# Score products over 128 rows, and a later place for one group of splits in the passage to the feed-forward

## The chip, the cores and the metric

The kernel runs on one core of a Trainium2 chip. The core has five engines with an instruction stream each: TensorE (PE in the profile; its weight loads are listed as PEld), VectorE (DVE), ScalarE (ACT), GpSimd (POOL) and SyncE (SP, which here only issues DMAs). They wait for each other by semaphores. The metric is the device time of one execution in microseconds (us), lower is better; the time of a kernel is the median over its runs.

## The reference, cut to what matters

One layer of a hybrid encoder, for 1024 new tokens behind 16 learned meta tokens (one sequence) and 32 further tokens with a cache of 256. A token mixer has three parts (forgetting attention with 6 heads of 64, pooling, a state-space scan), whose outputs go through one output projection; then comes a gated feed-forward. The change touches the scores of the attention and the start of the feed-forward:

```
def fox_block(q, k, v, c_q, c_k, q_pos, k_pos):
    s = jnp.einsum('bqhd,bkhd->bhqk', q, k).astype(jnp.float32) * (HD_FOX ** -0.5)
    s = s + jnp.transpose(c_q, (0, 2, 1))[:, :, :, None] - jnp.transpose(c_k, (0, 2, 1))[:, :, None, :]
    p = jax.nn.softmax(jnp.where(mask, s, -jnp.inf), axis=-1)
    return jnp.einsum('bhqk,bkhd->bqhd', p.astype(v.dtype), v)
...
    h = rmsnorm(x, ln_pre_ffn)
    ff = (jax.nn.silu(h @ w_gate) * (h @ w_up)) @ w_down
```

All is float32.

## The kernel before

**Split numbers.** TensorE multiplies in a format (fp32r) that keeps fewer bits than float32. So every operand is split into a high part (ScalarE copies it with rounding) and a low part (VectorE or GpSimd subtracts the high part from the original), and a product of two matrices is three products: high by high, high by low, low by high (`PASSES`).

**Scores.** A head has 64 channels, so the scores of a head contract over 64 rows only. The kernel stacks the parts: `K` holds the keys' high part in rows 0 to 63 and their low part in rows 64 to 127; `Q` holds the queries' high part in both halves. One product `Q` by `K` over 128 rows thus gives high by high and high by low together. The third term, queries' low part `QL` by the keys' high part, is a second product over 64 rows. `prep(h)` loads a head's operands into one tile `H` by ten DMAs of SyncE (keys, queries, `QL`, the bias `bc`, the values V) and counts up the planner's guess of when they have landed.

**One head** has 9 tiles of queries (48 rows, then eight of 128 rows), whose keys are cut into chunks of at most 512 columns: 15 chunks a head, 90 in all. For a chunk `s_products` issues the first product (`s`, 128 rows), then for a chunk that touches the diagonal a product that adds the mask (`am`, 128 columns or what of them lies in the chunk), and last the second product. VectorE adds the bias and takes the minimum (`s_min`, line 1029), ScalarE takes the exponential (`s_exp`, line 1040), TensorE transposes the result (`t`, line 1075), ScalarE and VectorE split it (`PT`, lines 58 and 63), TensorE multiplies by V (`o`), ScalarE evicts (`ot`).

**Order.** The loop over the chunks records, in each of its turns, one chunk's products, one group of transposes, the products of an earlier group, and then as many products of other work as a planner's clock allows: first the projections of the following heads (`wk`), later partial sums of the output projection (`wp`). The planner's clock, the guessed arrivals of DMAs and the `yield`s of `prep` fix the order of all five engines when the kernel is built; at run time each engine only works off its stream, in that order.

**The passage.** After the output projection the first two units of the feed-forward are computed with products that need no sums of weights (`first_units`, tiles `gc` and `gd`), while the last tokens are still normalised, transposed (`c_turns`) and split into the slots of `T`. `prep()` splits the next weight: ScalarE the high part, VectorE the low part. `c_parts(off, n)` splits `n` columns of the second half of the tokens (two splits) and forms two differences of the blocks (`c_diffs`, lines 1350 and 1351). The last weight of unit 1 is split into a place in `H2`, a tile of a pool that is opened there; its reader is the second half of `rows(1, 1, 0)` (`gc<-T,H`). `wx` is the weight before it, and `gd` are the products of the same units with the second half of the tokens.

Of the kernel before, what the change touches and what calls it, by code (L numbers as in the profile page):

```python
# [15 lines left out]
P = 128  # L16
D = 1024
NK = 8
NT = 1072
# [3 lines left out]
KEYS = PAST + NT  # L23
# [27 lines left out]
def tile_hybrid_trunk(ctx: ExitStack, tc: tile.TileContext, a: dict):  # L51
# [16 lines left out]
    def mm(out, lhsT, rhs, start, stop):  # L68
        return nc.tensor.matmul(out, lhsT, rhs, start=start, stop=stop, skip_group_check=True)  # L69
# [28 lines left out]
    def psum(tag, name):  # L98
        return where.get(tag, psp[0]).tile([P, 512], F32, tag=tag, bufs=PSB[tag], name=name)
# [14 lines left out]
    qd = [dr.tile([2, P, NT], F32, name=f"qd{p}") for p in range(3)]  # L114
# [7 lines left out]
    cd = dr.tile([6, KEYS], F32, name="cd")  # L122
# [110 lines left out]
    for t in range(9):  # L233
        R, o = TROW[t], TOFF[t]
# [4 lines left out]
        ps = zps[t]  # L239
# [98 lines left out]
    def cv_tile(tag, name):  # L338
        return CV.tile([P, EW], F32, tag=tag, bufs={"ext": 2, "cv": 4}[tag], name=name)
# [53 lines left out]
    for b in range(3):  # L393
        c0, n = CH[b]
        ps = psum("sm", f"ft{b}")
        for t in CTILES[b]:
            R, c = TROW[t], TOFF[t] - c0
# [47 lines left out]
    for i in range(5):  # L445
# [9 lines left out]
        h = cv_tile("cv", f"ch{i}")[:, :W]  # L455
# [19 lines left out]
    def arrival(nbytes):  # L475
        queue[0] = max(queue[0], clock[0]) + nbytes / 330.0
        return queue[0] + LATE[0]
# [333 lines left out]
    live, n = [], 0  # L811
# [27 lines left out]
    def prep(h):  # L839
        pr, hb = h // 2, 64 * (h % 2)  # L840
        H = (HB if h % 2 else HA).tile([P, HW], F32R, tag="H", name=f"H{h}")

        K, Q, QL = H[:, :KEYS], H[:, KEYS:KEYS + NT], H[:64, KEYS + NT:KEYS + 2 * NT]
        bc = H[:, KEYS + 2 * NT:2 * KEYS + 2 * NT]
        V = H[:, 2 * KEYS + 2 * NT:HW - P].rearrange("p (t c) -> p t c", c=P)
        Vm = H[:, HW - P:]
        heads[h] = (Q, QL, K, V, Vm, bc)
        v = vd[pr][:, h % 2].rearrange("r d j -> r (d j)")
        hs = slice(hb, hb + 64)
        loads = [(K[:64], kd[pr][0, hs]), (Q[:64], qd[pr][0, hs]), (K[64:], kd[pr][1, hs]), (Q[64:], qd[pr][0, hs]),  # L850
                 (QL, qd[pr][1, hs]), (bc, cd[h].partition_broadcast(P)),
                 (V[:, 0:2], v[0:PAST].rearrange("(t p) c -> p t c", p=P)), (V[:48, 2], v[PAST:PAST + 48]),
                 (Vm, v[PAST + 48 - P:PAST + 48]),
                 (V[:, 3:], v[PAST + 48:].rearrange("(t p) c -> p t c", p=P))]
        for i, (dst, src) in enumerate(loads):
            sync.dma_start(dst.bitcast(F32), src)
            at = arrival(4 * P * (KEYS if i == 5 else NT if i == 9 else KEYS // 2))
            if i % 2:
                yield
        ready[h] = at  # L860
# [113 lines left out]
    def geom(t):  # L974

        return TROW[t], TOFF[t], (0 if t == 0 else PAST + NS), (304 if t == 0 else NM + P * t)
# [13 lines left out]
    def place(t):  # L990

        free = [i for i in ring if SW[i] >= PAD + geom(t)[3]]
        return free[-1] if free else None

    def s_products(h, u, t, j, nch):
        Q, QL, K, V, Vm, bc = heads[h]
        R, o, k0, Lk = geom(t)
        if j == 0:
            st = AT.tile([P, 4], F32, tag="st", bufs=6, name=f"st{h}_{t}")
            i = place(t)  # L1000
            ring.remove(i)
            tiles[h, t] = (Sring[i], st)
            slot[h, t] = i
            if t in (0, 1, 3, 5, 7):
                i = 2 * ((5 * h + u) % 4)
                rows[h, u] = rsum[:, i:i + 2]
        j0 = 512 * j
        n = min(512, Lk - j0)
        ps = psum("s", f"s{h}_{t}_{j}")
        ks = slice(k0 + j0, k0 + j0 + n)  # L1010
        mm(ps[:R, :n], Q[:, o:o + R], K[:, ks], True, False)
        if t == 0:
            mm(ps[:R, :n], identr[:R, :R], am0, False, False)
        else:
            d0 = max(Lk - P, j0)
            d1 = j0 + n
            if d1 > d0:
                mm(ps[:R, d0 - j0:d1 - j0], identr, am[:, d0 - (Lk - P):d1 - (Lk - P)], False, False)
        mm(ps[:R, :n], QL[:, o:o + R], K[:64, ks], False, True)
        return ps  # L1020

    def s_min(h, u, t, j, nch, ps):
# [101 lines left out]
    while ti < len(Tgroups) or tolo or toprod or toout or later:  # L1124
# [31 lines left out]
        if tv:  # L1156
            for hi, lo, v in tv[1]:
                hi_of(hi, v)
            h, u, g, ng = tv[0]
# [8 lines left out]
        if s:  # L1168
            s_min(*s[0], s[1])
            h, u, t, j, nch = s[0]  # L1170
# [148 lines left out]
    def h_block(q):  # L1319
        return HT[:, q].rearrange("p (k n) -> p k n", k=4)  # L1320
# [19 lines left out]
    def c_parts(off, n):  # L1340

        for b in range(2):
            x = h_block(2 * b + 1)[:, :, off:off + n]
            split(*[t_slot(4 + 2 * b + j)[:, :, off:off + n] for j in range(2)], x)
        c_diffs(off, n)

    def c_diffs(off, n):

        b11, b12, b22 = [h_block(q)[:, :, off:off + n] for q in (0, 1, 3)]
        dv.tensor_tensor(out=b11, in0=b12, in1=b11, op=SUB)  # L1350
        dv.tensor_tensor(out=b12, in0=b22, in1=b12, op=SUB)
# [13 lines left out]
    def split(hi, lo, raw, eng=None):  # L1365
        hi_of(hi, raw)
        (eng or dv).tensor_tensor(out=lo, in0=raw, in1=hi.bitcast(F32), op=SUB)  # L1367
# [4 lines left out]
    def t_slot(m):  # L1372

        return T[:, m % 2, 4 * (m // 2 % 2):4 * (m // 2 % 2) + 4, CHN * (m // 4):CHN * (m // 4) + CHN]
# [67 lines left out]
    at = {"prep": 0, "raw": 0, "load": 0}  # L1442
# [121 lines left out]
    for t in range(9):  # L1564
        ks = (3, 4) if t < 2 else (0, 1, 2, 3, 4)
# [39 lines left out]
    def part_psums(nm):  # L1605

        turns[0] += 1
        return [psum(("mm", "sm")[turns[0] % 2], f"{nm}_{h}") for h in range(2)]
# [10 lines left out]
    def classic(f, q, ps, c, last):  # L1619

        w = W["gu", f, -(2 * q[0] + q[1] + 1)]
        for h in range(2):
            s = PART[h]
            n = s.stop - s.start
            for k in range(4):
                for j, (i0, i1) in enumerate(PASSES):
                    o = t_slot(4 * c + 2 * q[1] + i1)
                    mm(ps[h][:, :n], w[:, i0, k * P:(k + 1) * P], o[:, k, s],
                       q[1] == 0 and k == 0 and j == 0, last and k == 3 and j == 2)
        if c:  # L1630
            used(W.pop(("gu", f, -(2 * q[0] + q[1] + 1))))
# [219 lines left out]
    def first_units():  # L1851

        def rows(f, r, c, between=None):
            ps = part_psums(f"gc{f}_{r}_{c}")
            for m in range(2):
                classic(f, (r, m), ps, c, m == 1)
                if between and not m:
                    between()
            return ps

        for _ in range(3):
            prep()
        c_norms(9)
        prep()
        gate = rows(0, 0, 0)
        c_parts(0, 144)
        c_turns(7)
        prep()
        prep()
        up = rows(0, 1, 0)  # L1870
        c_norms(10)
        c_parts(144, 128)
        prep()
        classic_out(m1, gate, up)
        nc.gpsimd.dma_start(actd[0, :, 0], m1)
        gate = rows(1, 0, 0, lambda: c_turns(8))
        c_parts(272, 128)
        C.release()
        FX = tc.alloc_tile_pool(name="FX", bufs=1, side="right")
        H2pool[0] = FX  # L1880
        H2[0] = FX.tile([P, 6, SLOT], F32R, name="H2")

        w8 = H2[0][:, 5, :1024].rearrange("p (j c) -> p j c", j=2)
        places.append(w8)
        once.append(w8)
        prep()
        up = rows(1, 1, 0)
        classic_out(u2, gate, up)
        nc.gpsimd.dma_start(actd[1, :, 0], u2)
        ps = {(f, r): part_psums(f"gd{f}_{r}") for f in range(2) for r in range(2)}  # L1890
        b12, t1, t2, t3, t4, b22 = [act_out(0, i) for i in (0, 5, 6, 7, 4, 3)]
        for m in range(2):
            for f in range(2):
                for r in range(2):
                    classic(f, (r, m), ps[f, r], 1, m == 1)
                    if m and r:
                        classic_out((b12, b22)[f], ps[f, 0], ps[f, 1])
                        if f == 0:
                            dv.tensor_tensor(out=t1, in0=b12, in1=m1, op=SUB)
                    next(hgen)  # L1900
                    prep_more()
        dv.tensor_tensor(out=t2, in0=b22, in1=t1, op=SUB)
        dv.tensor_tensor(out=t3, in0=b22, in1=b12, op=SUB)
        dv.tensor_tensor(out=t4, in0=u2, in1=t2, op=SUB)
        nc.gpsimd.dma_start(actd[2, :, 0], t1)
        nc.gpsimd.dma_start(actd[3:7, :, 0].rearrange("s p n -> p s n"),
                            HT[:, 3].rearrange("p (s n) -> p s n", n=CHN))
# [205 lines left out]
```

## Time and profile before

| what | value |
|---|---|
| median of 3 runs | 1263.66 us (1263.57 to 1264.64) |
| the profiled execution, its own time | 1267.12 us |
| its span in the profile | 1265.3 us |
| granted TensorE clock, mean | 0.988 |
| TensorE busy with products | 1224.8 us (97% of the span) |
| VectorE busy | 843.5 us (67%) |
| ScalarE busy | 501.0 us (40%) |
| DMA queue of SyncE | 191.57 MB, 47.0% of 16 engines' span |

"Busy" is the time in which an engine has at least one instruction under way. A product's duration in the profile overlaps with the next one's, since products are pipelined, so what one costs is read from the start of one to the start of the next. In a timeline row the first number is the start, the second the time that the merged instructions span; `128*128 128x512` is a weight of 128 rows by 128 columns, moved over by 512 columns. What stands in brackets is the engine's idle time before, if it is over 0.15 us, and what ended it ("issue": nothing that the profile shows). The attention lies between 240 and 472 us of the span, the passage between 547 and 622 us.

### The profile page before, as it was taken

The numbers are of one execution on the slowest core, as the hardware profiler recorded it, in microseconds if no ns is written. First come the engines' busy times: TensorE is split into PE (matmuls) and PEld (weight loads), VectorE is DVE, ScalarE is ACT, GpSimd is POOL, SyncE is SP. The second block draws the span as 40 slices with busy tenths as digits, with TensorE's granted clock in tenths as the row PEclk, the third lists the DMA queues.
The fourth block names the chain that finished last, engine by engine and source line by source line (L and its number), as shares of the span: only waits on it lengthen the run. The fifth ranks groups of instructions, "written<-read, shape, count | busy, mean of one in ns | idle before, by whom it ended". The sixth has DMA issues, their size and how long they took to land.

```text
span 1265.3 us, 22956 instructions
## 1 busy us (share of the span) xinstructions
PE 1224.8 (97%) x8780; PEld 1146.1 (91%) x8780; DVE 843.5 (67%) x1620; ACT 501.0 (40%) x1104; POOL 193.2 (15%) x303
## 2 busy tenths in 40 slices
PE   7999899999999999889899999999999999999997
PEld 6999888888877776679899999999999999999996
DVE  4488687267676455675877777777777767555576
ACT  7422254245466562552432323223232335444432
POOL 0100386200122342440000000000000000000022
PEclk9999999999989999998999999999999999999998
DMA  9421264766665836551243444344433578655544
GB/s 299 148 82 55 63 175 151 243 199 182 200 193 174 262 109 229 201 168 67 77 137 138 171 145 162 133 151 154 167 128 137 196 273 302 243 187 181 186 145 148
DMA packets 128478, 213.85 MB, mean 169 GB/s; under 512 B 16227, under 2 KB 82857, under 8 KB 128369
## 3 DMA queue, kind: packets, MB, share of 16 engines
q1 hardware_dynamic: 123056, 191.57, 47.0%
q0 software_dynamic: 5312, 20.82, 4.3%
q8 instruction: 69, 1.13, 0.4%
q14 instruction: 41, 0.33, 0.1%
HBM read 144.66 MB, written 67.69 MB: 168 GB/s over the span
## 4 chain that ended last, share of the span: by engine, by line
PE 49%; DVE 1%; DMA 0%; issue 0%; ACT 0%; DVEq 0%; ACTq 0%
PE dn L69 14%; PE gy L69 14%; PE gz L69 9%; PE gx L69 9%; PE dl L69 3%; PE eT L1801 0%; DMA wsd<-ws 0%; DVE H L1367 0%; DVE ey L1831 0%; DVE HD L1367 0%; PE eT L1814 0%; DVE ey L1816 0%; DVE m L1663 0%; DVE T L1367 0%; DVE HT L1693 0%
## 5 line engine op out<-in xcount | busy, mean ns | idle before, releaser
L69 PE MATMUL wk<-T,wkh 128*128 128x384 f32 (+1 forms) x1152 | 205.2, 330 | 1.5 <-POOL wkh L66 0.8
L69 PEld LDWEIGHTS wk<-T,wkh 128*128 128x128 f32 x1152 | 186.8, 189 | 4.8 <-POOL wkh L66 1.1
L69 PE MATMUL gx<-T,HD 128*128 128x272 f32 (+1 forms) x960 | 120.5, 285 | 2.3 <-ACT m L1642 2.3
L69 PEld LDWEIGHTS gx<-T,HD 128*128 128x128 f32 x960 | 118.4, 188 | 2.5 <-ACT m L1642 2.5
L69 PE MATMUL gy<-H,HD 128*128 128x272 f32 (+1 forms) x960 | 119.3, 283 | 1.4 <-DVE m L1663 1.4
L69 PEld LDWEIGHTS gy<-H,HD 128*128 128x128 f32 x960 | 117.4, 188 | 1.6 <-DVE m L1663 1.6
L1367 DVE TENSOR_TENSOR HD<-rg,HD 128x512 fp32r<-128x512 f32 x126 | 86.1, 685 | 39.3 <-ACT HD L58 39.3
L69 PE MATMUL dn<-T,HD 128*128 128x272 f32 (+1 forms) x816 | 101.0, 285 | 0.4 <-DVE m L1663 0.4
L69 PEld LDWEIGHTS dn<-T,HD 128*128 128x128 f32 x816 | 100.1, 188 | 0.7 <-DVE m L1663 0.6
L69 PE MATMUL dn<-T,W 128*128 128x272 f32 (+1 forms) x768 | 94.7, 284 | 0.2 <-DVE W L1367 0.2
L69 PEld LDWEIGHTS dn<-T,W 128*128 128x128 f32 x768 | 93.9, 188 | 0.4 <-DVE W L1367 0.4
L1663 DVE TENSOR_TENSOR m<-gy,m 128x272 f32<-128x272 f32 x120 | 51.8, 432 | 48.8 <-PE gy L69 47.5
L58 ACT ACTIVATE HD<-rg 128x512 fp32r<-128x512 f32 x126 | 74.5, 624 | 18.5 <-PE gy L69 17.8
L58 ACT ACTIVATE PT<-t 128x512 fp32r<-128x512 f32 (+2 forms) x96 | 44.7, 472 | 90.1 <-PE t L1075 35.4
L1699 POOL DMA_DIRECT2D actd<-HT x20 | 15.3, 766 | 391.7 <-DVE HT L1675 273.8
L58 ACT ACTIVATE HD<-scr 128x512 fp32r<-128x512 f32 x20 | 12.7, 636 | 154.3 <-DVE scr L1498 154.3
L63 DVE TENSOR_TENSOR PT<-t,PT 128x512 fp32r<-128x512 f32 (+2 forms) x96 | 50.1, 527 | 31.9 <-ACT PT L58 31.0
L69 PE MATMUL s<-H 64*128 64x512 f32 (+5 forms) x180 | 65.0, 373 | 0.0
L69 PE MATMUL gy<-T,HD 128*128 128x272 f32 (+1 forms) x480 | 61.8, 285 | 0.0
L69 PE MATMUL gz<-T,HD 128*128 128x272 f32 (+1 forms) x480 | 61.6, 284 | 0.0
L69 PE MATMUL gz<-H,HD 128*128 128x272 f32 (+1 forms) x480 | 61.2, 283 | 0.0
L1367 DVE TENSOR_TENSOR T<-HT,T 128x528 fp32r<-128x528 f32 (+2 forms) x83 | 57.9, 704 | 4.9 <-ACT T L58 4.9
(309 smaller groups left out, 2276.3 us busy)
## 6 DMA issues: line engine op xcount, KB each, us to landing
rg<-in_wgu_dram SPq DMA_DIRECT2D x44, 512.0 KB
HT<-actd SPq DMA_DIRECT2D x77, 264.0 KB
actd<-HT POOLq DMA_DIRECT2D x11, 1056.0 KB, 5.7
ws<-in_wd_dram SPq DMA_DIRECT2D x44, 256.0 KB
wsd<-ws SPq DMA_DIRECT2D x44, 256.0 KB
rd<-wsd SPq DMA_DIRECT2D x20, 512.0 KB
wkr<-in_wx_dram SPq DMA_DIRECT2D x16, 512.0 KB
actd<-HT POOLq DMA_DIRECT2D x10, 792.0 KB, 4.0
```

Source lines behind the costliest of these rows:

```text
L58: nc.scalar.activation(out, in_, AF.Copy)
L63: nc.vector.tensor_tensor(out=out, in0=in_, in1=hi.bitcast(F32), op=ALU.subtract)
L69: return nc.tensor.matmul(out, lhsT, rhs, start=start, stop=stop, skip_group_check=True)
L1367: (eng or dv).tensor_tensor(out=lo, in0=raw, in1=hi.bitcast(F32), op=SUB)
L1663: return lambda h, ps: dv.tensor_tensor(out=out[:, PART[h]], in0=ps, in1=other[:, PART[h]], op=ADD)
L1699: nc.gpsimd.dma_start(actd[r0:r0 + n, :, p].rearrange("s p n -> p s n"), HT[:, 2 * (p % 2) + 1 - q, CHN * s0:CHN * (s0 + n)].rearrange("p ...
```

## The change

The second product of the scores is taken over 128 rows: `QL`, the queries' low part, is loaded twice, into rows 0 to 63 and 64 to 127, and is multiplied by the whole `K` (high and low part). The result so gets the term low by low as well. That is one DMA more for each of the six heads (64 by 1072 float32), so `prep` has eleven loads, and the planner counts the time of one more. In the passage `c_parts(272, 128)` stands behind the last `prep()` of unit 1, where it stood ahead of it.

```
-        K, Q, QL = H[:, :KEYS], H[:, KEYS:KEYS + NT], H[:64, KEYS + NT:KEYS + 2 * NT]
+        K, Q, QL = H[:, :KEYS], H[:, KEYS:KEYS + NT], H[:, KEYS + NT:KEYS + 2 * NT]
...
-                 (QL, qd[pr][1, hs]), (bc, cd[h].partition_broadcast(P)),
+                 (QL[:64], qd[pr][1, hs]), (QL[64:], qd[pr][1, hs]), (bc, cd[h].partition_broadcast(P)),
...
-            at = arrival(4 * P * (KEYS if i == 5 else NT if i == 9 else KEYS // 2))
+            at = arrival(4 * P * (KEYS if i == 6 else NT if i == 10 else KEYS // 2))
...
-        mm(ps[:R, :n], QL[:, o:o + R], K[:64, ks], False, True)
+        mm(ps[:R, :n], QL[:, o:o + R], K[:, ks], False, True)
...
         gate = rows(1, 0, 0, lambda: c_turns(8))
-        c_parts(272, 128)
         C.release()
...
         prep()
+        c_parts(272, 128)
         up = rows(1, 1, 0)
```

The planner's count of arrivals moves the order of the whole attention a little. At its end, on TensorE, this is the run from the last head's last scores to the output projection; in the kernel before (`t_4_0` to `t_4_4` are the groups of transposes of the last two query tiles, `o_4` their products, `wp` the partial sums):

```order
L69 MATMUL o_3_5072<-PT_3_3_5088,H_4460 128x128 x2
L69 MATMUL wp_1_5131<-wo_3421,T 128x512 x3
L1075 MATMUL t_4_1_5135<-ident,S_2392 128x128
L1075 MATMUL t_4_1_5135<-ident,S_2390 128x128
L1075 MATMUL t_4_1_5135<-ident,S_2392 128x128
L1075 MATMUL t_4_1_5135<-ident,S_2390 128x128
L69 MATMUL wp_1_5131<-wo_3730,T 128x512 x3
L69 MATMUL wp_1_5131<-wo_3861,T 128x512 x3
L1075 MATMUL t_4_2_5154<-ident,S_2392 128x128
```

In the changed kernel the same run on TensorE reads:

```order
L69 MATMUL o_3_5095<-PT_3_3_5112,H_4468 128x128 x2
L1075 MATMUL t_4_1_5150<-ident,S_2392 128x128
L1075 MATMUL t_4_1_5150<-ident,S_2390 128x128
L1075 MATMUL t_4_1_5150<-ident,S_2392 128x128
L1075 MATMUL t_4_1_5150<-ident,S_2390 128x128
L1075 MATMUL t_4_2_5164<-ident,S_2392 128x128
```

The nine `wp` products that stood between these transposes have gone to earlier places. In the passage, on ScalarE, the kernel before has this order (`yT` are the transposed last tokens, `T<-HT` the high parts of `c_parts(272, 128)`, `H<-rg` the high part of the last weight of unit 1):

```order
L1338 ACTIVATE HT<-yT_1_6084 128x4x128
L58 ACTIVATE T<-HT 128x4x128 x2
L58 ACTIVATE H_6129<-rg_1_5742 128x512
L1637 ACTIVATE m_5891<-gc_0_0_0_6053 128x272
L1637 ACTIVATE m_5891<-gc_0_0_1_6054 128x256
```

and the changed one:

```order
L1338 ACTIVATE HT<-yT_1_6090 128x4x128
L58 ACTIVATE H_6129<-rg_1_5748 128x512
L58 ACTIVATE T<-HT 128x4x128 x2
L1637 ACTIVATE m_5897<-gc_0_0_0_6059 128x272
L1637 ACTIVATE m_5897<-gc_0_0_1_6060 128x256
```

The weight's high part is now ahead of the tokens'. On VectorE the same place reads, before (`T<-HT` the low parts, `HT<-HT` the two differences, `H<-rg` the low part of the weight):

```order
L63 TENSOR_TENSOR T<-yT_1_6084,T 128x4x128
L1367 TENSOR_TENSOR T<-HT,T 128x4x128 x2
L1350 TENSOR_TENSOR HT<-HT 128x4x128
L1351 TENSOR_TENSOR HT<-HT 128x4x128
L1367 TENSOR_TENSOR H_6129<-rg_1_5742,H_6129 128x512
```

and in the changed kernel:

```order
L63 TENSOR_TENSOR T<-yT_1_6090,T 128x4x128
L1367 TENSOR_TENSOR H_6129<-rg_1_5748,H_6129 128x512
L1367 TENSOR_TENSOR T<-HT,T 128x4x128 x2
L1350 TENSOR_TENSOR HT<-HT 128x4x128
L1351 TENSOR_TENSOR HT<-HT 128x4x128
```

The weight's low part has moved ahead of four instructions of `c_parts`.

## Rows read from the trace of the kernel before

**Rows 1.** The page's first part: busy time of each engine in us, its share of the span, and the number of its instructions.

```profile
PE 1224.8 (97%) x8780; PEld 1146.1 (91%) x8780; DVE 843.5 (67%) x1620; ACT 501.0 (40%) x1104; POOL 193.2 (15%) x303
```

**Rows 2.** Busy time by stretch, for three stretches of the attention (with `wk` products between, with none, with `wp` products between). Columns: stretch, its length, busy us and number of instructions of PE, PEld, DVE, ACT and POOL, the granted share of TensorE's clock, the mean busy share of the DMA engines, GB/s.

```profile
240.00:343.00 103.00, 103.00 (x649) 89.49 (x647) 64.92 (x166) 48.09 (x130) 12.37 (x10) 1.00 0.63 186
343.00:372.00 29.00, 27.24 (x159) 21.08 (x157) 24.14 (x61) 18.79 (x48) 7.41 (x6) 0.88 0.65 198
372.00:464.00 92.00, 92.00 (x522) 71.38 (x521) 53.48 (x130) 53.70 (x129) 28.49 (x34) 1.00 0.64 191
```

**Rows 3.** The list of waits between 235 and 465 us: who waited for whom, us in total, how often, the longest one.

```profile
DVE S L1029 <- PE s L69: 42.6, 45, 5.2
...
PEld s L69 <- issue: 11.5, 42, 0.4
...
PEld t L1075 <- issue: 7.5, 32, 0.4
...
PEld o L69 <- issue: 2.4, 10, 0.2
...
PE t L1063 <- DVE T L63: 1.0, 1, 1.0
...
PE wk L69 <- POOL wkh L66: 0.8, 1, 0.8
...
PE wk L69 <- ACT wkh L58: 0.7, 1, 0.7
PE t L1075 <- ACT S L1040: 0.7, 1, 0.7
```

**Rows 4.** The timeline of TensorE's products at the start of the fifth head: a masked chunk of 272 columns, the first chunk of 512 columns (masked over 112), and the one of 16.

```profile
394.12 0.85 PE L69 MATMUL wp<-wo,T 128*128 128x512 f32 x3
394.82 0.29 PE L69 MATMUL s<-H 128*128 128x272 f32 x1
394.94 0.22 PE L69 MATMUL s<-am,identr 128*128 128x128 f32 x1
395.09 0.39 PE L69 MATMUL s<-H 64*128 64x272 f32 x1
395.41 0.33 PE L1075 MATMUL t<-ident,S 128*128 128x128 f32 x1
...
398.36 0.39 PE L69 MATMUL s<-H 128*128 128x512 f32 x1
398.58 0.21 PE L69 MATMUL s<-am,identr 128*128 128x112 f32 x1
398.73 0.50 PE L69 MATMUL s<-H 64*128 64x512 f32 x1
399.15 0.66 PE L1075 MATMUL t<-ident,S 128*128 128x128 f32 x4
399.57 0.42 PE L69 MATMUL o<-PT,H 128*128 128x128 f32 x2
...
400.57 0.17 PE L69 MATMUL s<-H 128*128 128x16 f32 x1
400.60 0.26 PE L69 MATMUL s<-am,identr 128*128 128x16 f32 x1
400.78 0.27 PE L69 MATMUL s<-H 64*128 64x16 f32 x1
400.99 0.33 PE L1075 MATMUL t<-ident,S 128*128 128x128 f32 x1
```

**Rows 5.** The timeline at a chunk of 512 columns without a mask, weight loads included (the two products of the chunk are one row, the second starts with its weight load at 457.64).

```profile
457.09 0.19 PEld L69 LDWEIGHTS s<-H 128*128 128x128 f32 x1
...
457.32 0.82 PE L69 MATMUL s<-H 128*128 128x512 f32 x2
...
457.64 0.18 PEld L69 LDWEIGHTS s<-H 64*128 64x128 f32 x1 [0.36 <-issue]
...
458.07 0.66 PE L1075 MATMUL t<-ident,S 128*128 128x128 f32 x4
```

**Rows 6.** The weight loads of the tile of scores `s` in the view of one tile: count, shortest, median and longest duration in ns, first and last start, and their forms with counts.

```profile
L69 PEld LDWEIGHTS s<-H x180: 119/183/338, 240.2 to 460.5; 128*128 128x128 f32 x84, 64*128 64x128 f32 x84, 128*48 128x48 f32 x6, 64*48 64x48 f32 x6
```

**Rows 7.** The timeline of the passage around the last weight of unit 1 (`H<-rg`) and its reader (`gc<-T,H`).

```profile
576.28 1.14 ACT L58 ACTIVATE T<-HT 128x512 fp32r<-128x512 f32 x2
576.93 1.29 DVE L1367 TENSOR_TENSOR T<-HT,T 128x512 fp32r<-128x512 f32 x2 [1.19 <-ACT T L58]
577.32 0.61 ACT L58 ACTIVATE H<-rg 128x512 fp32r<-128x512 f32 x1
...
577.99 0.52 PE L69 MATMUL gc<-T,H 128*128 128x272 f32 x2 [0.73 <-ACT H L58]
...
578.86 0.69 DVE L1351 TENSOR_TENSOR HT<-HT 128x512 f32<-128x512 f32 x1
579.47 0.69 DVE L1367 TENSOR_TENSOR H<-rg,H 128x512 fp32r<-128x512 f32 x1
580.21 5.19 PE L69 MATMUL gc<-T,H 128*128 128x272 f32 x22 [1.70 <-DVE H L1367]
...
585.20 9.47 PE L69 MATMUL gd<-T,HD 128*128 128x272 f32 x72
```

**Rows 8.** Busy time by stretch, columns as in Rows 2, just behind that.

```profile
580.00:585.00 5.00, 4.79 (x22) 4.79 (x23) 0.60 (x2) 0.00 (x0) 0.00 (x0) 0.50 0.31 105
```

## Prediction

> **What bounds the kernel now.** I read the page's busy times first [rows 1]: TensorE has a product under way for 97% of the span, VectorE works 67% of it, ScalarE 40%. That makes TensorE the first suspect everywhere, but says nothing yet on whether its products are as dense as they could be. So I went to the attention, where the first edit lies, by stretch [rows 2]: TensorE is busy 103.00 of 103 us and 92.00 of 92 us, and VectorE there only 64.92 and 53.48. The list of waits says the same from the other side [rows 3]: between 235 and 465 us TensorE's products waited for another engine four times, 3.2 us in all, while VectorE alone waited 42.6 us for the scores. Only the stretch from 343 to 372 us, in which no foreign products fill the gaps, is different: VectorE is busy 24.14 of 29 us, and TensorE no longer all the time [rows 2]. The reader is to see that in 203 of 232 us an instruction that TensorE saves shortens the span, and in 29 us hardly.
>
> The same list shows something odd [rows 3]: the unit that loads weights stood idle ahead of loads for scores 42 times, 11.5 us, behind nothing that the profile knows ("issue"), and as oddly ahead of transposes (7.5 us) and of products by V (2.4 us). Elsewhere it loads the next weight under the running product. The timeline shows where [rows 4, 5]: each idle piece stands at the change from a product over 128 rows to the one over 64, or back.
>
> **The first edit: what a second product costs.** I take starts, not durations, and compare each step with what it takes between products of 128 rows. The references: three `wp` products of 512 columns take 0.70 us, 0.23 each; 272 columns take 0.12; and two products with a weight each are never less than about 0.11 apart, which the four transposes show (0.42 for four) [rows 4].
> - 512 columns without a mask: from the first product to the second 0.32 us, from the second to the transposes 0.43 [rows 5]. Over 128 rows I expect 0.23 each, so 0.29 less.
> - 512 columns with a mask: 0.15 from the mask to the second product, 0.42 from there on [rows 4]. Expected 0.11 and 0.23: 0.23 less.
> - 272 columns: 0.15 and 0.32 [rows 4]. Expected 0.11 and 0.12: 0.24 less. Chunks of 144 and 400 columns have the same two changes, and I price them alike.
> - 16 columns: 0.18 and 0.21 [rows 4]. Expected 0.11 twice: 0.17 less.
> - The first query tile of a head: its mask product has 48 rows and stays so, so the change of rows only moves from behind the second product to ahead of it: nothing.
>
> There are 84 second products with 64 rows by 128 columns, and 6 of the last kind [rows 6]. By the widths of the keys a head has six chunks of 512 columns, two of them masked, and two each of 16, 144, 272 and 400. So: 24 x 0.29 = 7.0; 12 x 0.23 = 2.8; 36 x 0.24 = 8.6; 12 x 0.17 = 2.0; together **20.4 us**. The idle time of the weight loads at "issue" is the same thing counted from the other side, 11.5 + 7.5 + 2.4 = 21.4 us [rows 3], and serves as the upper bound.
>
> What takes from it. (a) In the stretch from 343 to 372 us VectorE has 24.14 us of work [rows 2]. That stretch's share of the 20.4 by length is 2.6 us, which would leave 26.4 us, with VectorE busy 91% of it and itself behind ScalarE's splits. I take 2.0 of the 2.6 as lost. (b) At the end of the attention the order has taken nine `wp` products out from between the last transposes. They cost 9 x 0.23 = 2.1 us wherever they stand, but they covered the time in which the splits are made. The price lies between nothing and 2.1; I take 1.0, since ScalarE and VectorE go on splitting meanwhile. (c) The six added DMAs carry 0.27 MB each; at 186 GB/s [rows 2] that is 1.5 us of transfer a head, next to DMA engines that are 63 to 65% busy. They lie a head ahead of their use and cost the path nothing. Queued behind each on SyncE are the bias and the values of the same head and the writes of earlier results; nobody waits for a DMA in the list [rows 3]. If that cover went, it would be 1.5 us a head, 9 us in all. (d) The planner's shift moves when other products fill the gaps, not how many there are. I price it at nothing, between the 2.1 us of (b) lost once more and as much gained. So the first edit brings **17.4 us**, between 12 (20.4 less 2.6, 2.1, 1.5 for one head at (c), and 2.1) and 21.4.
>
> **The second edit.** In the passage TensorE reaches `gc<-T,H` at about 577.1 us and waits 0.73 us for the weight's high part, does two products, and waits 1.70 us for its low part [rows 7]. ScalarE makes the high part at 577.32 behind the two token splits of `c_parts`; VectorE makes the low part at 579.47 behind two token splits and two differences [rows 7]. In the new order the high part takes the tokens' place at 576.28 and ends at 576.9; VectorE follows at about 576.95 and ends at 577.64. TensorE gets to the third product at 577.3 or so and can go on at 577.7 instead of 580.21: **2.5 us**. What is late next is `c_parts` itself: 0.6 us later on ScalarE, its low parts end near 578.9 and its differences at 580.3. Their first reader is the second half of `gd`, not before TensorE has done 22 more products, 2.7 us; it is covered, and if it were not, it would cost what is missing of that, under 1 us.
>
> Then the clock. From 580 to 585 us the granted clock is 0.50, the lower of the two levels (1.2 GHz instead of 2.4) [rows 8]: 22 products take 4.99 us [rows 7], where 24 of the `gc` kind at full clock take about 0.12 each, 2.7 in all. Before it fell TensorE had stood idle for 2.4 of 3.2 us. Without these waits I expect no fall there, which gives back 2.3 us up to 585.2 and some 0.7 in `gd`, **3.1 us**. The price lies between 0 (it falls all the same) and 3.1; I take 3.1, since the idle time ahead of it is nearly gone. The second edit thus brings 5.6 us, between 2.5 and 5.6.
>
> **Sum.** The profiled execution took 1267.12 us; 17.4 + 5.6 = 23.0 less is 1244.1. It lies 3.46 us above the median of the runs, 1263.66, so against these the forecast is 1240.7, rounded **1241 us**.
>
> **Rivals.**
> 1. Row count is not what costs. The second product is also the last of its group, and the time could lie in that place, or in the reading of `H`. Against it: `wp` and `o` products that end a group show no such step [rows 4], and both the step in and the step out are there at chunks with and without a mask. For it: the weight loads of both kinds take the same time, 0.19 and 0.18 us [rows 5]. Then only the second edit is left: 1263.66 - 2.5 to 5.6, about 1259 us. Chance 0.06. The Trainium skill speaks for this rival: "TensorE: Matmul & The Clock Gate", section "LDWEIGHTS (loading the stationary operand)", says that a load's time goes by its columns and that 32 rows load as slowly as 128. By that rule alone the sum would be without its 20.4 us. The trace agrees on the loads, but not on the steps between products, and these I trust.
> 2. VectorE and ScalarE take TensorE's place. Half of the 20.4 us turns into waits of TensorE for exponentials and splits. For it: the stretch of (a). Against it: 142.5 us of VectorE work in 224 us of these three stretches [rows 2]. Gain 10.2 + 2.5: 1251 us. Chance 0.17.
> 3. Slower than before: a head's scores wait for its loads. Heads follow each other sooner while each has more to load through the in-order queue of SyncE. To eat the whole 23 us, the five heads behind the first must each wait over 4.6 us. A head's loads are 3.2 MB, 17 us at 186 GB/s [rows 2]; if 5 us of that showed at each of the five, the time would be 1241 + 25 = 1266 us. Nothing in the list waits for a load of `H` [rows 3]. Chance 0.03.
> 4. More than forecast: the low clock in the stretch from 343 to 372 us (0.88 granted of 29 us is 3.5 us lost [rows 2]) goes too, and nothing is lost at (a) and (b): 21.4 + 5.6 + 3.5 = 30.5 less, 1233 us. Chance 0.08.
>
> **How the numbers follow.** My forecast has the remaining 0.66, with a range of its own from 1236 to 1247. The range for 8 in 10 reaches from rival 4's 1233 to the bounds on the other side: 12 + 2.5 us gained and one more fall of the clock, 3.5 us, is 11 us less, 1253. That includes rival 2 and leaves out rivals 1 and 3 and what lies beyond. A measurement of this kernel can tell about 0.2%, 2.5 us, from no change. Faster by more than that are the forecast, rivals 2 and 4, and most of rival 1 (0.04): 0.95. Rival 1's rest and a little of what stands between is no change, 0.03; slower is 0.02.
>
> **What would show it.** Right: in the profile of the changed kernel the step from a second product of 512 columns to the next one is 0.23 us, not 0.42; the idle weight loads at "issue" are gone from the list; the attention ends some 17 us sooner; `gc<-T,H` runs on with under 0.5 us of waits and at full clock. Wrong: TensorE waits over 5 us in all for VectorE or ScalarE in the attention (rival 2), or for DMAs to `H` (rival 3); the steps stay over 0.4 us (rival 1); or the clock falls at other places than now, 3.5 us each.

## The result, and the profile after

| kernel | median | runs | ratio to before, 95% interval |
|---|---|---|---|
| before | 1263.84 us | 1263.57 to 1264.64 | |
| changed | 1250.08 us | 1246.46 to 1253.17 | 0.9891, 0.9869 to 0.9912 |

The change saves 13.8 us, where 22.7 were forecast: the direction is right and the time lies inside the range, but two fifths of the gain are missing, and the narrower range of the forecast itself, 1236 to 1247 us, was missed. The profiled execution (1246.46 us, span 1244.7 us, mean granted clock 0.992) is the shortest of the changed kernel's four; that of before (1267.12 us) lay above its median. Between these two the difference is 20.7 us, so what the profiles show has to be held against the medians.

First the page's busy times, as [rows 1]: TensorE has 24.5 us less of work with the same number of products.

```profile
PE 1200.3 (96%) x8780; PEld 1141.0 (92%) x8780; DVE 841.6 (68%) x1620; ACT 500.2 (40%) x1104; POOL 194.9 (16%) x303
```

The steps are gone, as forecast. In the timeline of TensorE's products in the changed kernel stand a masked chunk of 272 columns, four transposes behind a chunk of 512, a masked chunk of 512, one of 16, and (last) one of 512 without a mask, as [rows 4, 5]:

```profile
383.23 0.29 PE L69 MATMUL s<-H 128*128 128x272 f32 x1
383.35 0.22 PE L69 MATMUL s<-am,identr 128*128 128x128 f32 x1
383.41 0.34 PE L69 MATMUL s<-H 128*128 128x272 f32 x1
383.59 0.27 PE L1075 MATMUL t<-ident,S 128*128 128x128 f32 x1
...
387.74 0.60 PE L1075 MATMUL t<-ident,S 128*128 128x128 f32 x4
388.10 0.42 PE L69 MATMUL o<-PT,H 128*128 128x128 f32 x2
...
402.37 0.40 PE L69 MATMUL s<-H 128*128 128x512 f32 x1
402.61 0.21 PE L69 MATMUL s<-am,identr 128*128 128x112 f32 x1
402.65 0.45 PE L69 MATMUL s<-H 128*128 128x512 f32 x1
402.95 0.27 PE L1075 MATMUL t<-ident,S 128*128 128x128 f32 x1
...
449.06 0.17 PE L69 MATMUL s<-H 128*128 128x16 f32 x1
449.09 0.26 PE L69 MATMUL s<-am,identr 128*128 128x16 f32 x1
449.20 0.26 PE L69 MATMUL s<-H 128*128 128x16 f32 x1
449.31 0.33 PE L1075 MATMUL t<-ident,S 128*128 128x128 f32 x1
```

```profile
439.62 0.42 PEld L69 LDWEIGHTS s<-H 128*128 128x128 f32 x2
439.85 0.62 PE L69 MATMUL s<-H 128*128 128x512 f32 x2
440.09 0.58 PEld L1075 LDWEIGHTS t<-ident,S 128*128 128x128 f32 x4
440.32 0.49 PE L1075 MATMUL t<-ident,S 128*128 128x128 f32 x3
```

Read by starts: from the mask product to the transposes 0.24 us (272 columns; before 0.15 + 0.32), 0.34 (512; before 0.15 + 0.42) and 0.22 (16; before 0.18 + 0.21); from the first product of an unmasked chunk to the transposes 0.47 (before 0.32 + 0.43). In the last fence the weight loads lie under the running products again, where [rows 5] has the one for 64 rows begin only at 457.64, after 0.36 us of idle time. The idle time of the weight loads at "issue" between 235 and 465 us, 21.4 us in [rows 3], is 2.7 us here. With the counts of the prediction the starts give 24 x 0.28 + 12 x 0.23 + 36 x 0.23 + 12 x 0.17 = 19.8 us.

These starts end at the first transpose, and a part of the step lies behind it. Four transposes behind a chunk of 512 columns take 0.42 us in [rows 4] (399.15 to 399.57) and 0.36 here (387.74 to 388.10). By the medians over all chunks it is 0.04 to 0.06 us at each width but 16 columns, some 4 us more, so that the steps are worth about 24 us in all.

The waits, though, have grown. These are TensorE's own in the list of waits of the changed kernel between 235 and 465 us (who waited for whom, us in total, how often, the longest):

```profile
PE wp L69 <- ACT pp L938: 2.6, 1, 2.6
PE o L69 <- ACT ot L1113: 2.0, 4, 0.8
PE o L69 <- DVE PT L63: 1.9, 3, 0.8
PE wk L69 <- DVE k L572: 1.2, 1, 1.2
PE sT L888 <- issue: 0.9, 1, 0.9
PE wk L69 <- POOL wkh L66: 0.8, 1, 0.8
PE wk L69 <- ACT wkh L58: 0.5, 1, 0.5
PE t L1075 <- ACT S L1040: 0.5, 2, 0.2
PE t L1075 <- DVE T L63: 0.4, 1, 0.4
```

That is 10.8 us against 3.2 in [rows 3] (3.8 if the attention of before is followed to its end at 472 us). The longest is new and of a kind that the prediction did not have: TensorE waits until ScalarE has emptied a bank of partial sums into the buffer `pp`. The timeline there, DMA issues included:

```profile
398.52 0.58 ACT L938 ACTIVATE pp<-wp 128x512 f32<-128x512 f32 x1
...
412.69 0.32 SPq L940 DMA_DIRECT2D ppd<-pp  x1
...
417.79 0.60 ACT L938 ACTIVATE pp<-wp 128x512 f32<-128x512 f32 x1 [4.33 <-DMA ppd<-pp]
...
418.44 1.43 PE L69 MATMUL wp<-wo,T 128*128 128x512 f32 x3 [2.60 <-ACT pp L938]
```

ScalarE stood idle for 4.33 us, and what released it was a store of an earlier content of `pp`. There are two such buffers, so it is by their order the store issued at 412.69. What it stores was complete when the eviction of 398.52 ended: it was issued 13.6 us later, behind loads of the next head and other transfers in SyncE's stream, and freed its buffer only by 417.79, another 5.1 us later. Behind that wait the clock falls. By stretch (length, then busy us and instructions of PE, PEld, DVE, ACT and POOL, granted clock, DMA share, GB/s), first there and then in the passage:

```profile
416.00:424.00 8.00, 5.50 (x17) 4.19 (x18) 1.09 (x2) 3.15 (x8) 3.00 (x5) 0.79 0.73 254
```

```profile
560.00:568.00 8.00, 7.83 (x65) 7.61 (x64) 5.95 (x10) 3.23 (x8) 0.56 (x1) 1.00 0.29 107
```

The passage itself went as forecast. Its timeline, as [rows 7]:

```profile
561.22 0.62 ACT L58 ACTIVATE H<-rg 128x512 fp32r<-128x512 f32 x1
561.75 1.14 ACT L58 ACTIVATE T<-HT 128x512 fp32r<-128x512 f32 x2
561.88 0.69 DVE L1367 TENSOR_TENSOR H<-rg,H 128x512 fp32r<-128x512 f32 x1 [1.18 <-ACT H L58]
...
562.05 0.41 PE L69 MATMUL gc<-T,H 128*128 128x272 f32 x2
...
562.63 2.94 PE L69 MATMUL gc<-T,H 128*128 128x272 f32 x22 [0.16 <-DVE H L1367]
```

Waits of 0.73 and 1.70 us have become 0.16, and the 22 products take 2.8 us at a clock of 1.00 (562.63 to 565.41, where `gd` starts), where [rows 7, 8] had 4.99 us at 0.50.

### The profile page after: what moved, and what is told of

The parts are those of the page before. It is cut to its first block, busy times and chain, and to the rows that moved or that the text cites. A ratio compares the mean times of both kernels' runs of the same rounds, so it can differ in the third digit from the quotient of the medians.

```text
span 1244.7 us, 22979 instructions
## 1 busy us (share of the span) xinstructions
PE 1200.3 (96%) x8780; PEld 1141.0 (92%) x8780; DVE 841.6 (68%) x1620; ACT 500.2 (40%) x1104; POOL 194.9 (16%) x303
## 4 chain that ended last, share of the span: by engine, by line
PE 49%; DVE 1%; DMA 1%; issue 0%; ACT 0%; DVEq 0%; SPq 0%; ACTq 0%
PE dn L69 15%; PE gy L69 13%; PE gx L69 9%; PE gz L69 9%; PE dl L69 3%; DMA HT<-actd 1%; PE eT L1801 0%; DMA wsd<-ws 0%; DVE HD L1367 0%; DVE H L1367 0%; DVE ey L1831 0%; PE eT L1814 0%; DVE m L1663 0%; DVE T L1367 0%; DVE ey L1816 0%
## 5 line engine op out<-in xcount | busy, mean ns | idle before, releaser
L69 PE MATMUL o<-PT,H 128*128 128x256 f32 (+1 forms) x324 | 59.2, 297 | 4.1 <-ACT ot L1113 2.0
L69 PEld LDWEIGHTS gy<-T,HD 128*128 128x128 f32 x480 | 60.0, 189 | 0.0
```

## The experiments

Each time stands beside runs of the kernel before on the same chip, and the ratio is to these; one hundredth in the ratio is 12.6 us. With single ratios known to 0.1 to 0.3 hundredths, a difference of two is uncertain by some 2 to 5 us. The kernel before itself scattered more there than in the runs above, from 1259.33 to 1273.31 us, with granted clocks from 0.993 to 0.984.

| run | order | added transfer | rows | passage | median, us | ratio (95%) |
|---|---|---|---|---|---|---|
| e1 | old | yes | 128 | old | 1250.06 | 0.9875 (0.9848 to 0.9902) |
| e2 | old | no | 64 | new | 1261.72 | 0.9971 (0.9950 to 0.9992) |
| e3 | new | yes, not read | 64 | new | 1263.90 | 0.9991 (0.9973 to 1.0009) |
| e4 | old | yes | 128 | new | 1246.79 | 0.9848 (0.9820 to 0.9876) |
| e5 = changed | new | yes | 128 | new | 1249.18 | 0.9883 (0.9864 to 0.9901) |
| e6 | old | no, zeros | 128 | new | 1240.47 | 0.9821 (0.9802 to 0.9840) |
| e7 | old | yes; sums by GpSimd | 128 | new | 1243.02 | 0.9838 (0.9818 to 0.9858) |
| e8 | old | yes | 96 | new | 1247.46 | one run |
| e9 | old | no, zeros; sums by GpSimd | 128 | new | 1242.05 | 0.9828 (0.9815 to 0.9842) |
| e10 | old | yes, not read | 64 | new | 1261.79 | 0.9982 (0.9971 to 0.9992) |
| e11 | old | no, zeros | 128 | old | 1245.42 | 0.9846 (0.9832 to 0.9860) |
| e12 | old | no | 64, swapped | old | 1271.86 | one run |

The theory at the start: the steps belong to the row count and are worth what was forecast; the missing 9 us are waits that the new order brought. The rivals: the gain is the order's (rival 1), or the shorter products meet waits whatever the order (rival 2).

**e1, the 128 rows in the old order.** The second transfer is issued with the first and the planner doesn't count it, so that TensorE, VectorE and ScalarE run the order of before.

```
-            sync.dma_start(dst.bitcast(F32), src)
+            for d in ((dst, QL[64:]) if i == 4 else (dst,)): sync.dma_start(d.bitcast(F32), src)
...
-        mm(ps[:R, :n], QL[:, o:o + R], K[:64, ks], False, True)
+        mm(ps[:R, :n], QL[:, o:o + R], K[:, ks], False, True)
```

> The kernel before with the second product over 128 rows alone: queries' low part is loaded twice, but the planner doesn't count the added transfer, so that the order of TensorE, VectorE and ScalarE is that of before; the passage is as before. Theory (a change of the row count between products is what costs): the 84 steps get shorter by 20.8 us in the sum of the start-to-start times, and some 3 us come back as waits, so 1246 us against 1263.8. Rival 1 (the row count costs nothing, the new order of the changed kernel brought the gain): 1262 to 1264. Rival 2 (waits for exponentials and splits eat half of it whatever the order): 1253.

1250.06 us. The gain is not the order's: rival 1 falls. It is smaller than expected: the time lies half way between the theory (1246) and rival 2 (1253). TensorE's wait for `pp` is here too, 3.2 us.

**e2, the passage alone.**

```
-        c_parts(272, 128)
         C.release()
...
         prep()
+        c_parts(272, 128)
```

> The kernel before with the passage's edit alone. Theory: 2.5 us of waits and one fall of TensorE's clock (3 us) go, 1258 us. Rival (the fall comes all the same, a little later, or is not there in most runs of the kernel before): 1261 us.

1261.72 us, 3.2 less than the 1264.88 of before. That is nearer to the rival (2.8 less than 1263.8) than to the theory (5.8 less), but the interval, 1 to 6 us, holds both. In the profile the clock is 1.00 at the place of the edit (572 to 580 us). It falls at an earlier one instead, where that of before is at 1.00:

```profile
558.00:566.00 8.00, 6.37 (x38) 5.94 (x37) 6.23 (x10) 6.94 (x14) 3.64 (x5) 0.79 0.59 197
```

**e3, the changed kernel with 64 rows.**

```
-        mm(ps[:R, :n], QL[:, o:o + R], K[:, ks], False, True)
+        mm(ps[:R, :n], QL[:64, o:o + R], K[:64, ks], False, True)
```

> The changed kernel with its order and its eleven loads, but the second product of the scores over 64 rows again (the doubled load of the queries' low part is made and not read). Theory: the steps at the changes of the row count come back (0.42 us from a second product of 512 columns to the transposes), 20.8 us in all, of which the waits that the changed kernel shows in the attention (10 us against 3.8 before) hide some; the new order by itself costs between 0 and 3 us. So 1258 to 1262 us. Rival 1 (the gain is from the order): 1250 us as the changed kernel. Rival 3 (the new order by itself costs 6 us, the longer waits being all its own): 1264 us.

1263.90 us. The new order and the transfer eat what the passage's edit gave (0.9991 against 0.9971), 2.5 us. Row count alone separates this kernel from the changed one: 0.9991 against 0.9891, 12.6 us.

**e4, both edits in the old order** (the edits of e1 and e2 together).

> Both edits with the order of before (the added transfer isn't counted by the planner). Theory A (the 2.6 us wait for the eviction of a partial sum at 415 us of the changed kernel, and a part of the other waits, come from the order): 1241 to 1243 us, 7 us under the changed kernel's median. Theory B (whatever the order, the products that are now shorter meet the same waits): 1250 us as the changed kernel.

1246.79 us, between the two expectations, and the sum of e1 and e2 (0.9875 + 0.9971 - 1 = 0.9846). Theory A's reason falls: the wait for `pp` is there in the old order as well, 2.2 us. The first two of TensorE's waits between 235 and 465 us:

```profile
PE wp L69 <- ACT pp L938: 2.2, 1, 2.2
PE wk L69 <- ACT wkh L58: 1.7, 1, 1.7
```

So a new theory: the added transfer itself delays other DMAs, the stores of partial sums and the raw weights of the projections (`wkr`, from which ScalarE makes `wkh`).

**e5, the changed kernel again.**

> The changed kernel once more, on the chip of the next three. It differs from e4 (both edits, old order) only in the order that the counted transfer brings. If the new order costs what e3 showed against e2 (2.2 us between the medians), 1249 us; if the order costs nothing, 1247 us as e4. Nothing but the order differs, so any difference above 1.5 us is its price.

1249.18 us, 0.9883 against 0.9848 for e4, 4.4 us, on different chips. The profiles don't show it: the span is 1245.1 us here and 1245.0 in e4, and TensorE's waits in the attention add up to 9.7 and 9.3 us. But the profiled execution of e5 (1246.91 us) is 2.3 us shorter than its median, so what its other runs lost is not to be seen in it.

**e6, zeros in place of the transfer.** This computes what the kernel before does (the low by low term is zero).

```
-        Vm = H[:, HW - P:]
+        Vm = H[:, HW - P:]; nc.gpsimd.memset(QL[64:].bitcast(F32), 0.0)
...
-            for d in ((dst, QL[64:]) if i == 4 else (dst,)): sync.dma_start(d.bitcast(F32), src)
+            sync.dma_start(dst.bitcast(F32), src)
```

> e4 (both edits, old order) without the added transfer: rows 64 to 127 of the queries' low part are set to zero by GpSimd, so the result has no low by low term, as before; products, order and row counts are those of e4. Theory A (the added 0.27 MB a head, in front of the stores in SyncE's queue, is what makes the partial sum's store land late, so that ScalarE waits 4.5 us for it and TensorE 2.2): the wait falls under 1 us, and the clock's fall behind it goes too, 1243 us. Theory B (the wait comes from the shorter products alone, which reach the store's buffer sooner): 1247 us as e4.

1240.47 us, the shortest median of all. Both waits shrink, `pp` from 2.2 to 0.8 and `wkh` from 1.7 to 0.3 (the same list):

```profile
PE wp L69 <- ACT pp L938: 0.8, 1, 0.8
...
PE wk L69 <- ACT wkh L58: 0.3, 1, 0.3
```

The clock does not fall there, which the same stretch shows, in e4 and then in e6:

```profile
416.00:424.00 8.00, 5.75 (x21) 3.94 (x20) 0.27 (x1) 2.56 (x6) 1.81 (x3) 0.79 0.82 289
```

```profile
416.00:424.00 8.00, 8.00 (x42) 6.26 (x41) 2.88 (x11) 4.05 (x13) 1.08 (x2) 1.00 0.87 309
```

**e7, the partial sums' stores in GpSimd's queue.**

```
-                sync.dma_start(ppd[TOFF[t]:TOFF[t] + TROW[t]], st[:TROW[t]])
+                nc.gpsimd.dma_start(ppd[TOFF[t]:TOFF[t] + TROW[t]], st[:TROW[t]])
```

> e4 with the stores of the partial sums issued by GpSimd in its own queue, not behind the loads of the next head in SyncE's. Theory A (the store waits its turn in SyncE's queue): it lands soon, the 2.2 us wait and the clock's fall at 420 us go, 1242 to 1244 us. Theory B (the DMA engines are full at that place, so the store is as late by any queue): 1247 us. Rival against both: GpSimd's own work is held up behind the stores, 1250 us or more.

1243.02 us is in theory A's range, but by the ratios e7 is only 1.3 us under e4 (0.9838 against 0.9848), within the error: the time does not decide. The waits do. The one for `pp` is gone from the list (its first line is now `wkh`, 1.6 us), and in the same stretch the DMA engines are as full as ever while TensorE is busy throughout:

```profile
416.00:424.00 8.00, 8.00 (x40) 6.27 (x39) 0.91 (x4) 3.35 (x9) 3.79 (x6) 1.00 0.99 322
```

The store is now issued 0.3 us behind its eviction:

```profile
403.73 0.59 ACT L938 ACTIVATE pp<-wp 128x512 f32<-128x512 f32 x1
404.62 0.58 POOL L940 DMA_DIRECT2D ppd<-pp  x1 [11.66 <-ACT pp L938]
```

The same store is issued 9.9 us behind it in e4 (eviction at 402.64, issue at 413.10) and 8.4 in e6 (399.83 and 408.82). So the place in SyncE's stream makes the store late, not a lack of bandwidth, and the added transfer is a part of what stands ahead.

**e8, 96 rows.**

```
-        mm(ps[:R, :n], QL[:, o:o + R], K[:, ks], False, True)
+        mm(ps[:R, :n], QL[:96, o:o + R], K[:96, ks], False, True)
```

> e4 with the second product over 96 rows (32 rows of the low by low term are left out). Theory A (TensorE pays when a product uses half of the rows or less and the next one more): 96 rows cost no step, 0.23 us from a second product of 512 columns to the next product, 1247 us as e4. Theory B (any change of the row count costs): steps of 0.42 us as with 64 rows, 1262 us.

1247.46 us (one run), and no step: for a masked chunk of 272 columns the starts are 0.06 and 0.18 us apart, as with 128 rows. A change between 128 and 96 rows is free, one between 128 and 64 is not.

```profile
439.53 0.22 PE L69 MATMUL s<-am,identr 128*128 128x128 f32 x1
439.59 0.34 PE L69 MATMUL s<-H 96*128 96x272 f32 x1
439.77 0.27 PE L1075 MATMUL t<-ident,S 128*128 128x128 f32 x1
```

**e9, e6 and e7 together.**

> e6 (zeros in place of the added transfer, both edits, old order) and also the partial sums' stores on GpSimd's queue as in e7. Theory: the 0.76 us wait of TensorE for a partial sum that e6 has left goes too, 1239 to 1240 us. Rival (the two kernels remove the same thing): 1240.5 us as e6.

1242.05 us, 0.9828 against 0.9821: no further gain, although the wait for `pp` is gone. The two remove the same thing.

**e10, the transfer alone**, 64 rows in the old order (e4 with the product of before).

> The kernel before with the passage's edit (e2) and the added transfer, made and not read: second product over 64 rows, old order. Theory A (the transfer costs by itself: weights of the projections before the first head and stores of partial sums come later): e2 plus 2 to 5 us, ratio to before 1.000. Theory B (it costs only where the products are shorter): as e2, ratio 0.997.

0.9982 against 0.9971 for e2: 1.4 us, between the theories, and within the error. The profile names a price: TensorE's wait for `wkh` ahead of the first head is 1.7 us as in e4, 0.3 in e2. There is no wait for `pp`. At its full length that wait takes both, the transfer and the shorter products; with one of them it is 0.8 to 0.9 us (e6 and e11 without the transfer, e3 with 64 rows in the new order) or none.

**e11, e6 without the passage's edit.**

> e6 without the passage's edit: what the second edit is worth where nothing of the first depends on transfers. Theory (2.5 us of waits in every run, and a fall of the clock at that place that is worth up to 3 us in some of them): e6 plus 3.2 us as e2 measured, 1243.7 us, ratio to before 0.985. Rival (the fall at that place is there in all runs): e6 plus 5.6, 1246 us.

0.9846 against 0.9821 for e6: 3.2 us for the second edit, the third time (0.9875 to 0.9848 from e1 to e4 is 3.4), each with an error of 3 us or more. Against before, e11 is the row count alone: 0.9846 is 19.5 us (17.7 to 21.2). The clock falls behind `gc<-T,H` as before, but for less: 0.79 over 8 us, where before has 0.57 (579.5 to 587.5),

```profile
559.00:567.00 8.00, 6.31 (x39) 6.24 (x39) 3.75 (x7) 0.05 (x1) 0.56 (x1) 0.79 0.20 66
```

and 0.79 at that place in e1 too, which is 0.21 x 8 = 1.7 us.

**e12, the two products of before in the other order**, the one over 64 rows first.

```
-        mm(ps[:R, :n], Q[:, o:o + R], K[:, ks], True, False)
+        mm(ps[:R, :n], QL[:, o:o + R], K[:64, ks], True, False)
...
-        mm(ps[:R, :n], QL[:, o:o + R], K[:64, ks], False, True)
+        mm(ps[:R, :n], Q[:, o:o + R], K[:, ks], False, True)
```

> The kernel before with the two products of the scores in the other order: queries' low part by keys' high part first, over 64 rows, the mask, and the product over 128 rows last. Theory (the row count costs, wherever the product stands): the last product goes on to the transposes after 0.23 us, and the first, over 64 rows, takes the step instead, 0.09 us more ahead of it and 0.19 behind it; the time is that of before, 1261 to 1265 us. Rival 1 (the place as last of its group costs): the last product still takes 0.42 us.

The step moved with the 64 rows. In the timeline with weight loads (one unmasked chunk) the load for 64 rows begins at 457.46 after 0.37 us of idle time and the one for 128 rows 0.42 us later, at 457.88:

```profile
457.46 0.18 PEld L69 LDWEIGHTS s<-H 64*128 64x128 f32 x1 [0.37 <-issue]
457.46 0.93 PE L69 MATMUL s<-H 64*128 64x512 f32 x2
457.88 0.19 PEld L69 LDWEIGHTS s<-H 128*128 128x128 f32 x1 [0.24 <-issue]
458.01 0.57 PEld L1075 LDWEIGHTS t<-ident,S 128*128 128x128 f32 x4
458.22 0.60 PE L1075 MATMUL t<-ident,S 128*128 128x128 f32 x4
```

The place as last of its group does not cost 0.42: rival 1 is out here too. Not as expected are the 0.34 us from the last product to the transposes (457.88 to 458.22), where 0.23 were expected, and the time of the one run, 1271.86 us. Where the mask product stands in between, the last product takes its usual time (0.18 us at 272 columns, 401.15 to 401.33). So the 0.34 seems to belong to the change from 64 rows to 128, a part of which reaches past the next product, as it does past the first transpose in the kernel before. By the medians of the starts, e12's chunks take 7 us more in all than those of before; its attention, from the first scores to the last product by V, takes 239.4 us against 231.2.

## Why the prediction was right, and where it was off

**TensorE as the bound, and the steps: right in kind, a little small.** 20.4 us forecast; by the same starts 19.8 were measured, and with what lies behind the first transpose about 24. The prediction missed that part because its own reference, 0.42 us for four transposes [rows 4], stands behind a product over 64 rows. So the idle time of the loads, 21.4 us, was no upper bound, and 0.11 us is not the least distance of two products either: [rows 4] has 0.03 (400.57 to 400.60). Where only the row count differs and there is no added transfer, the time shows 19.5 us (before to e11) and 19.0 (e2 to e6), where the first edit was to bring 17.4 after its losses.

e3 and e8 leave only the row count, and of that the change between 128 rows and 64. [rows 5] and the fence from 439.62 show how: over 128 rows the next weight is loaded under the running product; a load that changes the rows to 64 starts only behind it. The Trainium skill has a rule that bears on this, in "TensorEngine Tiling (Array Packing)", section "Key Properties": changing the tiling mode drains TensorE. The steps at 64 rows agree with that (0.42 us in place of 0.23), and so does the missing step at 96 rows, if 64 rows count as a mode of their own and 96 as the full array; no run here shows the modes themselves. The Trainium skill's rule on weight loads, which the prediction weighed, is right for the load (0.18 us against 0.19) and says nothing on the step around it.

**Losses (a) and (b): right.** (a), in the stretch where no products fill the gaps, was forecast at 2.0 us: TensorE's waits there are 3.6 us in e6 (330 to 357 us) and 1.7 before (343 to 372), 1.9 more. (b), at the end of the attention in the new order, was forecast at 1.0: the changed kernel waits 0.8 us for `ot` behind the last scores (454 us), and so do e3 and e5; e4, in the old order, does not.

**Loss (c), the added DMAs at nothing: the step that failed.** It said that the transfers "lie a head ahead of their use and cost the path nothing", and that "nobody waits for a DMA in the list". The first part holds for their reader: TensorE doesn't wait for `H` in the changed kernel either. The second is a misreading. The rows shown have no such wait, but the whole list of before, over the same 235 to 465 us, has several, and this one among them:

```profile
ACT pp L938 <- DMA ppd<-pp: 0.7, 1, 0.7
```

Before, it cost TensorE nothing. In the changed kernel it is 4.3 us, in e4 4.5, and TensorE waits behind it for 2.2 to 3.2 us in every run that has the transfer, a second product over 96 or 128 rows and the stores in SyncE's queue (changed, e1, e4, e5, e8). Without the transfer it waits for 0.8 to 0.9 (e6, e11). SyncE's queue carries what others wait for, and weights of the projections come 1.4 us later, too (e10 against e2, e4 against e6). Behind the wait for `pp` the granted clock was 0.64 to 0.79 over 416 to 424 us in all five profiles that have it at full length, and 1.00 in the same stretch of the other nine; 0.79 is another 0.21 x 8 = 1.7 us. By the ratios the transfer costs 3.4 us (e4 to e6), 3.7 (e1 to e11) and, with 64 rows, 1.4 (e2 to e10). None of the three is clear of its error alone; the first two together are (3.6, error about 3). The prediction did say what the transfers would cost without cover, 9 us at most.

**Loss (d), the planner's shift at nothing, between -2.1 and +2.1: the size and the place not settled.** By the ratios the new order costs 1.1 us (e10 to e3, within the error) and 4.4 (e4 to e5, just outside it). In the waits it shows as one for `k` of 1.2 us (changed, e3, e5), which no run in the old order has, and as four for `ot`, 2.0 us; but other waits are shorter, and the profiles' spans are equal. Where the time goes remains open. No run has the zeros of e6 in the new order, so what transfer and order cost together was not taken apart.

**The second edit: mechanism right, the clock mis-sized.** The waits were 2.43 us and are 0.16; the forecast 2.5 us holds. The clock's 3.1 us came from one profiled execution. In the profiles of e1 and e11 the fall at that place is 1.7 us. In the changed kernel and e2 to e10 the clock was 1.00 there: the fall did go. But in seven of these ten profiles (not in the changed kernel, e4 and e5) it fell at another place between 545 and 600 us, as in e2 above, which the prediction had named as a sign of being wrong (at 3.5 us each; here it is 0.79 over 8 us, 1.7). By the ratios the edit brings 3.2 to 3.7 us, not 5.6; the three estimates together are good to about 2 us.

**The sum.** e6 has 22.3 us less than before, which is the 22.7 of the forecast, from other parts: 19.0 to 19.5 us for the first edit and 3.2 for the second, in place of 17.4 and 5.6. That these two errors cancel is luck. What the changed kernel loses against e6 is the price of the transfer, 3.4 to 3.7 us, and of the order, 1.1 to 4.4: 19.5 + 3.2 less these is 14.6 to 18.2 us, and 13.8 and 14.8 were measured (changed kernel, e5). So the parts add up only with the higher price of the order.

**The rivals.** The time is that of rival 2 (1251 us), and its sign, over 5 us of waits for VectorE or ScalarE, was met in the list. Its cause was not: half of the steps did not turn into waits for exponentials and splits, as e6 and e11 show, which have these products and keep 19.0 to 19.5 us. Of e4's 9.3 us of waits, 2.8 more than e6's 6.5, the added part came with the transfer. Rival 3 named the right resource, the queue, with the wrong victim.

**Beyond both kernels:** e6 has 1240.47 us, ratio 0.9821 (0.9802 to 0.9840). It gets the full row count without a byte more to load.

## What to carry to other kernels

Where products over 128 rows and over 64 rows alternate, read the time from start to start: each pair of changes cost some 0.2 to 0.4 us here, and filling the half with zeros was at least as good as filling it with data. Price an added transfer not only by who reads it, but by everything behind it in its queue, stores that free a buffer above all, and read the whole list for waits of any engine for a DMA: a short one is where a longer one begins. A gain that rests on the granted clock of one profiled execution is worth what several executions show: here 1.7 of the 3.1 us in two others, and in most kernels with the edit the clock fell at another place instead.

## What the runs showed that was not expected

- A product over 96 rows next to ones over 128 costs no step, one over 64 rows 0.09 us on the way in and 0.2 on the way out (512 columns), and up to 0.06 more past the first product behind it.
- With the 64 rows first (e12), the product over 128 rows behind them took 0.34 us to the next one instead of 0.23; with the mask product in between it took its usual time. No other run tells how the step is shared out.
- The same kernel on the same chip scattered by 14 us (before, 23 runs, 1259.33 to 1273.31), with mean granted clocks from 0.984 to 0.993.
